# Buffer alignment in SBUF: probability buffers at multiples of 512 bytes, their transposed targets at multiples of 256, and one weight group moved to another pool

## The chip, the cores and the metric

The kernel runs on one core of a Trainium2 chip. Its five instruction streams are TensorE (PE, with its weight loads shown apart as PEld), VectorE (DVE), ScalarE (ACT), GpSimd (POOL) and SyncE (SP), which in this kernel does nothing but issue DMAs. Each stream runs its own instructions in order and waits for the others at semaphores. The metric is the time of one execution in microseconds of device time; runs are given by their median.

## The reference

One encoder layer over 2048 tokens of width 1024, in float32: `x + RMSNorm(W_out · ([A | B | M] * silu(z)))`. A, B and M all read one normalised input `h` through one combined projection.

```
h = rms_norm(x, norm_pre_w);  proj = h @ w_in
aq, ak, av, bqkv, ba, bb, mq, z = split(proj)
y_a = attention(rope(rms(aq)), rope(rms(ak)), av)        # 8 heads of 128, 2 key/value heads, 2048 x 2048
y_b = bidirectional gated DeltaNet(conv(bqkv), ba, bb)    # 4 heads, chunks of 64, both directions
y_m = attention(mq, keys and values from 256 memory tokens)  # 4 heads
x + rms_norm((concat(y_a, y_b, y_m) * silu(z)) @ w_out, norm_post_w)
```

The part that the change is about is the softmax attention: for each block of 128 queries and each head, scores of 128 x 2048, their softmax, and the product of the probabilities with the values.

## The kernel before, in words

Nearly every operation is recorded through a small wrapper, so that most of them stand at line 51 (L51) in the profile, and they are told apart by the names of their tiles. The weight loads issued by POOL stand at L77.

The kernel goes through its work in stages: the memory tokens' keys and values, the normalised tokens and the value projection (to about 122 us of the span), the key and query projections (to about 440), the projection and convolution of branch B (to about 700), the DeltaNet with the projections of `z` and `mq` between its steps (to about 1370), the attention (to about 2270) and the output projection (to the end).

Float32 precision is kept by splitting an operand in two halves, a high one and a low one: the float32 value rounded, and what is left. A product is then three matmuls (high·high, high·low, low·high).

**Attention.** There are 64 units (one head, 256 queries) of two blocks of 128 queries each, and 8 memory units of one block each, so 136 blocks. A block goes through these steps, and blocks overlap by up to five steps:

- PE computes the scores `sa` from the keys `K` and the queries `qa`; DVE takes their maximum (`mxa`); ACT exponentiates into the float32 tile `Pa`.
- `high()` has ACT write the high half of the normalised probabilities to `hla[:, 0]`; `low()` has DVE and POOL write the low half to `hla[:, 1]`. The tile `hl` (`hla`, for memory units `hlm`) is 128 partitions x 2 x 2048 half-precision numbers, 8 KB for each partition, in 3 buffers.
- SP then issues one transposing DMA at L1139, which writes the whole of `hla` into a quarter of the room `PT`, in 128 x 128 pieces. The four `PT` tiles hold two blocks each; PT0 and PT1 lie in the pool `hT`, PT2 and PT3 in the pool `late`.
- `value()` has PE multiply `PT` with the values `V` into `pva`; DVE multiplies the result by the gate (`gaa`), and SP stores it to the DRAM tensor `mix`.

PE, ACT and DVE run in an order written out by hand in this stage. SP's queue carries, besides the transposes, the loads of the queries (`qa<-qT`), of the gate (`gaa<-gate`), of memory queries (`M<-mqT`), and the stores (`mix<-gaa`).

**Pools.** The pool `hT` has one tag, `B16`, with 6 slots of 16 KB for each partition; in the course of the kernel they hold the raw weights (`wraw`), the turned memory tokens (`mT`), the turned tokens (`hT`), and in attention `K`, `V`, `M`, PT0, PT1, and parts of the output weights (`wo`) and of its input (`mhl`). Each is asked for with an alignment (`align_bytes`) of 128.

**Weight groups.** `load_w` loads a group of weight columns into `wraw`, squares it on ACT to find its scale (`wss`, `wsb`, a one-column matmul on PE, `wsc`), and splits it into half-precision parts (`wparts`) with ACT, DVE and POOL. Groups are counted by `n`. Group 0 has 272 columns (the values of A and the columns of `ba` and `bb`) and is loaded by SP while the memory groups are worked on; group 1 (256 columns) is the keys; groups 2 and on are queries and the rest. `parts` come from the pool `wpool` (tag `whb`, 2 buffers) for every third group beginning at 1, and otherwise from the pool `wp` (tag `whl`, 4 buffers), which the memory groups' parts (`whi`, `wlo`) use as well. Apart from the stages with pinned engines a scheduler orders the instructions of each engine, by its own estimate of when each is ready.

Of the kernel before, what the change touches and what calls it, by code (L numbers as in the profile page):

```python
# [11 lines left out]
F32 = mybir.dt.float32  # L12
F32R = mybir.dt.float32r
BF16 = mybir.dt.bfloat16
F16 = mybir.dt.float16
# [7 lines left out]
S = 2048  # L23
D = 1024
NMEM = 256
# [3 lines left out]
KC = D // 128  # L29
# [8 lines left out]
def hybrid_layer(ctx: ExitStack, tc: tile.TileContext, t: dict, out, dbg=None):  # L38
# [111 lines left out]
    def load_w(srcs, width, fac=(1.0,), fetch=None):  # L150


        n = wcount[0]
        wcount[0] += 1
        room = hpool.tile([128, 2, 4, width], F32, tag="B16", name="wraw", bufs=6, align_bytes=128)
        raws = [room[:, half] for half in range(2)]
        for half in range(2):
            for ap_to, ap_from in srcs(raws[half], half):
                (fetch or wdma)(ap_to, ap_from)
        pool, tag, bufs = (wpool, "whb", 2) if wpool is not None and n % 3 == 1 else (wp, "whl", 4)  # L160
        parts = [pool.tile([128, 2, 4, width], F16, tag=tag, name="wparts", bufs=bufs) for _ in range(2)]

        def small(name, dt=F32, pool=const2, bufs=4):
            return pool.tile([128, 1], dt, tag=name, name=f"{name}{n}", bufs=bufs)

        ss = [small(f"wss{i}") for i in range(2)]
        for half in range(2):
            A.activation(parts[half][:, 0].bitcast(BF16), raws[half], AF.Square, accum_out=ss[half])
        sb, y, e, sc = small("wsb", BF16), small("wy"), small("we", I32), small("wsc")
        V.tensor_tensor(sb, ss[0], ss[1], op=ALU.add)  # L170
        ps = tp_ps(f"wss{n}", (128, 1))
        T.matmul(ps, onesb, sb, start=True, stop=True)
        V.tensor_scalar(y.bitcast(I32), ps.bitcast(I32), -0.5, 1597463007.0, op0=ALU.mult, op1=ALU.add)
        V.tensor_scalar(e, y.bitcast(I32), 0x7f800000, None, op0=ALU.bitwise_and)
        V.tensor_scalar(sc.bitcast(I32), e, 1.0, float(14 << 23), op0=ALU.mult, op1=ALU.add)
        V.tensor_scalar(y.bitcast(I32), e, -1.0, float(240 << 23), op0=ALU.mult, op1=ALU.add)
        cs = [small("wc1", bufs=2)] * (len(fac) - 1) + [small("wc0", pool=const)]
        for c, f in zip(cs, fac):
            V.tensor_scalar(c, y, hcs, f, op0=ALU.mult, op1=ALU.mult)
        G.tensor_scalar(raws[1], raws[1], sc, None, op0=ALU.mult)  # L180
        A.activation(parts[0][:, 0], raws[0], AF.Copy, scale=sc)
        A.copy(parts[1][:, 0], raws[1])
        V.scalar_tensor_tensor(parts[0][:, 1], raws[0], sc, parts[0][:, 0], op0=ALU.mult, op1=ALU.subtract)
        G.tensor_tensor(parts[1][:, 1], raws[1], parts[1][:, 0], op=ALU.subtract)
        return [(w[:, 0], w[:, 1]) for w in parts], cs
# [3 lines left out]
    hpool = ctx.enter_context(tc.tile_pool(name="hT", bufs=1))  # L189
    p3 = ExitStack()  # L190
    wp = p3.enter_context(tc.tile_pool(name="wp", bufs=1))
# [7 lines left out]
    def tp_ps(name, shape=(128, 512)):  # L199
        return ps1.tile(list(shape), F32, tag="tp", name=name, bufs=4)  # L200

    hT = []
# [46 lines left out]
    wpool = w12.enter_context(tc.tile_pool(name="w12", bufs=1))  # L249

    def load_group(segs, fetch=None, fac=(1.0,)):

        def src(raw, half):
            o = 0
            for c0, n in segs:
                yield raw[:, :, o:o + n], t["w_in"][0, 512 * half:512 * half + 512, c0:c0 + n].rearrange("(k p) c -> p k c", p=128)
                o += n
        return load_w(src, sum(n for _, n in segs), fac, fetch)
# [12 lines left out]
    with tc.tile_pool(name="s0", bufs=1) as p:  # L271
# [15 lines left out]

        wmem = p.tile([128, D], F32, tag="wn", name="wmem")
        wpre = p.tile([128, D], F32, tag="wn", name="wpre")
        mTt = hpool.tile([128, 2, KC, NMEM], F32R, tag="B16", name="mT", bufs=6, align_bytes=128)  # L290
        mT = [mTt[:, i] for i in range(2)]
        xs, hm = [], []
        for j in range(2):
# [58 lines left out]
        for g in range(4):  # L352
# [2 lines left out]
                wav, (avcs,) = load_group([(1280, 256), (3072, 16)], dma)  # L355
            mem_group(g, wg)
            wg = nxt
        hT.extend(hpool.tile([128, 2, KC, 512], F16, tag="B16", name=f"hT{b}", bufs=6, align_bytes=128).rearrange("p i k c -> i p k c") for b in range(4))
        hs = {}

        def tok_norm(tb):
# [249 lines left out]
    wpool = None  # L611
# [48 lines left out]
                    (attention_loads, attention_slots)[b]()  # L660

    def slot(name, shape, dt=F32R):
        return hpool.tile(shape, dt, tag="B16", name=name, bufs=6, align_bytes=128)

    def late_slot(name, shape, dt=F32R):

        return late.tile(shape, dt, tag="L16", name=name, bufs=2, align_bytes=128)

    at = {}

    def attention_loads():

        at["k"] = slot("K", [128, 2, 2, S], F16)
        at["q0"] = wp.tile([128, 2, 2 * QW], F16, tag="wraw", name="qa0_0", bufs=1)
        dma(at["q0"], qT_d[0, :, :, 0:2 * QW])
        for k in range(4):
            dma(at["k"][:, 0, :, k * 512:(k + 1) * 512], kT_d[0, :, :, k * 512:(k + 1) * 512])

    def attention_slots():
        at["v"] = slot("V", [128, 2, TB, 256], F16)  # L680
        at["PT"] = [slot(f"PT{i}", [128, 2, 2, 16, 128], F16) for i in range(2)]
# [108 lines left out]
    with tc.tile_pool(name="s3a", bufs=1) as sv0:  # L790
        p = rows
# [24 lines left out]
        for hp in range(2):  # L816
            p = (sv0, sv1)[hp]
# [222 lines left out]
    late = ctx.enter_context(tc.tile_pool(name="late", bufs=1, side="right"))  # L1040
    ps2 = ctx.enter_context(tc.tile_pool(name="ps2", bufs=1, space=PSUM))
    p5 = ExitStack()
    p = p5.enter_context(tc.tile_pool(name="at", bufs=1))
# [7 lines left out]
    class Block:  # L1051
# [63 lines left out]
            V.reciprocal(sm[:, 2:3], sm[:, 2:3])  # L1115

        def high(self):
            hl = self.hl = p.tile([128, 2, S], F16, tag="hl", name=f"hl{self.nm}", bufs=3, align_bytes=128)
            P = self.P.rearrange("p a c -> p (a c)")
            if self.u["mem"]:  # L1120
                A.copy(hl[:, 0], P)
            else:
                A.activation(hl[:, 0], P, AF.Copy, scale=self.sm[:, 2:3])
            n = self.u["n"]
            if n in (2, 3) and len(PT) == n:
                PT.append(late_slot(f"PT{n}", [128, 2, 2, 16, 128], F16))
            self.pt = PT[n % 4][:, self.qb]
# [137 lines left out]
    for i in range(len(blocks) + LAG + 1):  # L1265
# [29 lines left out]
        for tb in range(2):  # L1295
            n = i - len(blocks) - 2 * tb
# [38 lines left out]
    with ExitStack() as es:  # L1335
        p = es.enter_context(tc.tile_pool(name="op", bufs=1))
        wo.append([late_slot(f"wo{i}_2", [128, 4, D]) for i in range(2)])
        wo.append([p.tile([128, 4, D], F32R, name=f"wo{i}_3") for i in range(2)])

# [98 lines left out]
```

## Time and profile before

| | |
|---|---|
| median of 3 runs | 2619.63 us (2618.19 to 2632.11) |
| the profiled execution | 2617.16 us, span 2615.4 us, mean granted clock of TensorE 0.972 |
| PE / PEld busy | 2393.9 us (92%) / 1626.0 us (62%) |
| DVE / ACT / POOL busy | 1754.0 us (67%) / 1285.6 us (49%) / 733.0 us (28%) |
| DMA | 440.08 MB, mean 168 GB/s, 857298 packets, 639744 of them under 512 B |
| largest idle times of PE by releaser | the transposing DMA into `PT` from `hla`: 96.0 us before `pva` |

PE is busy for 92% of the whole span. In the attention it is busy for less, and the 16 DMA engines are nearly always busy there (the row of DMA digits in the page has 9 in nearly every slice of this stage). A busy share of a window above 1 in the DMA column means that the packets' times overlap. SP's rows (SPq) are the time that its queue spent on issuing a DMA; they are not counted among the busy engines.

### The profile page before, as it was taken

How to read it: one execution, taken by the hardware profiler on the slowest of the kernel's cores; microseconds unless marked ns; L12 is line 12 of the kernel's file. 1: busy time of each engine (PE TensorE's matmuls, PEld its weight loads, DVE VectorE, ACT ScalarE, POOL GpSimd, SP SyncE). 2: the span in 40 equal slices, each digit the busy share in tenths (PEclk: the TensorE clock that was granted, in tenths of full speed). 3: DMA queues.
4: the chain of work that ended last, by engine and by line, in shares of the span. 5: the costliest groups of instructions: out<-in, count | busy, mean ns of one | idle time of the engine just before them, and what ended most of it. 6: DMA issues, size and time to landing. Idle time of an engine off the chain costs nothing.

```text
span 2615.4 us, 43108 instructions
## 1 busy us (share of the span) xinstructions
PE 2393.9 (92%) x15981; PEld 1626.0 (62%) x15981; DVE 1754.0 (67%) x3463; ACT 1285.6 (49%) x2496; POOL 733.0 (28%) x556
## 2 busy tenths in 40 slices
PE   7889999999999899999998888888888899999998
PEld 6778974555544356666645555555555555688887
DVE  7677769999568645545537777787887788442222
ACT  5633335544432245555636666676676677321110
POOL 2155331111202310210214444444455554200000
PEclk9999999999999999999999999998999999999999
DMA  6432223234585657767659999999999999953331
GB/s 206 152 92 86 65 62 101 73 113 131 192 254 126 191 166 215 235 207 233 215 173 221 211 212 208 213 213 205 195 213 211 210 207 203 218 164 95 96 95 51
DMA packets 857298, 440.08 MB, mean 168 GB/s; under 512 B 639744, under 2 KB 813184, under 8 KB 856832
## 3 DMA queue, kind: packets, MB, share of 16 engines
q1 hardware_dynamic: 844640, 394.32, 63.1%
q0 software_dynamic: 12448, 43.00, 4.9%
q8 instruction: 126, 2.06, 0.3%
q14 instruction: 84, 0.69, 0.1%
HBM read 186.62 MB, written 108.00 MB: 113 GB/s over the span
## 4 chain that ended last, share of the span: by engine, by line
PE 21%; issue 15%; POOL 12%; DMA 5%; DVE 2%; ACT 1%; SPq 1%; POOLq 0%; DVEq 0%; ACTq 0%
PE o L51 12%; POOL hla L51 7%; POOL Pa L51 4%; PE z L51 3%; DMA PT<-hla 2%; PE pva L51 1%; PE sa L51 1%; DMA xx<-bx 1%; DVE mxa L51 1%; DMA Od<-oo 1%; POOL wo L51 1%; DMA wor<-in_w_out 1%; DVE hla L51 1%; DMA ft<-FT 0%; PE sm L51 0%
## 5 line engine op out<-in xcount | busy, mean ns | idle before, releaser
L51 PE MATMUL pva<-PT,V 128*128 128x256 f16 x3072 | 399.0, 282 | 115.4 <-DMA PT<-hla 96.0
L51 PEld LDWEIGHTS <-wparts 128*128 128x128 f16 x3072 | 294.0, 98 | 326.4 <-issue 16.4
L51 PEld LDWEIGHTS <-V 128*128 128x128 f16 x3072 | 305.6, 101 | 225.0 <-issue 96.4
L51 ACT ACTIVATE Pa<-sa,mxa,undo 128x1024 f32<-128x1024 f32 x256 | 305.8, 1198 | 223.7 <-DVE sma L51 186.0
L51 DVE TENSOR_REDUCE mxa<-sa 128x1 f32<-128x1024 f32 x256 | 309.6, 1217 | 140.6 <-PE sa L51 139.5
L51 PE MATMUL sa<-K,qa 128*128 128x512 f16 x1536 | 388.4, 390 | 5.1 <-ACT Pa L51 3.6
L51 PE MATMUL z<-hT,wparts 128*128 128x512 f16 x1536 | 372.4, 383 | 0.0
L51 PE MATMUL o<-wo,mhl 128*128 128x512 f32 x1416 | 325.5, 391 | 3.9 <-ACT wo L51 2.6
L51 PEld LDWEIGHTS o<-wo,mhl 128*128 128x128 f32 x1416 | 265.4, 188 | 63.7 <-ACT wo L51 3.4
L51 ACT ACTIVATE hla<-Pa,sma 128x2048 f16<-128x2048 f32 x128 | 255.5, 1996 | 37.2 <-DMA PT<-hla 34.2
L51 DVE SCALAR_TENSOR_TENSOR hla<-Pa,sma,hla 128x1536 f16<-128x1536 f32 x128 | 258.4, 2018 | 5.9 <-ACT hla L51 5.9
L51 PE MATMUL b<-hT,wparts 128*128 128x512 f16 x1152 | 256.8, 379 | 0.0
L51 PEld LDWEIGHTS <-hT 128*128 128x128 f16 x2304 | 226.2, 99 | 38.3 <-ACT hT L51 5.9
L51 POOL TENSOR_TENSOR Pa<-Pa,sma 128x512 f32<-128x512 f32 x128 | 134.5, 1051 | 406.6 <-ACT hla L51 398.4
L51 PEld LDWEIGHTS <-qa 128*128 128x128 f16 x1536 | 154.7, 101 | 146.2 <-issue 21.6
L51 POOL TENSOR_TENSOR hla<-Pa,hla 128x512 f16<-128x512 f32 x128 | 229.4, 1792 | 9.4
L51 PE MATMUL q<-wparts,hT 128*128 128x256 f16 x1920 | 214.9, 274 | 0.0
L51 POOL TENSOR_SCALAR wraw<-wraw,wsc 128x1024 f32<-128x1024 f32 (+1 forms) x22 | 67.5, 3067 | 335.8 <-DVE wy L51 256.8
L51 DVE TENSOR_TENSOR mhl<-mr,mhl 128x2048 fp32r<-128x2048 f32 (+1 forms) x16 | 35.1, 2192 | 177.3 <-ACT mhl L51 177.2
L51 DVE SCALAR_TENSOR_TENSOR y<-xb,convw,y 128x512 f32<-128x512 f32 x192 | 145.5, 773 | 1.7
L51 ACT CAST mhl<-mr 128x2048 fp32r<-128x2048 f32 (+1 forms) x16 | 29.2, 1826 | 225.9 <-PE o L51 211.1
L77 POOL DMA_DIRECT2D gate<-zg x64 | 35.5, 555 | 367.9 <-DVE zg L51 197.8
(317 smaller groups left out, 3274.6 us busy)
## 6 DMA issues: line engine op xcount, KB each, us to landing
xx<-bx SPq DMA_DIRECT2D x64, 512.0 KB, 5.0
wraw<-in_w_in POOLq DMA_DIRECT2D x42, 512.0 KB, 5.3
gate<-zg POOLq DMA_DIRECT2D x64, 256.0 KB, 4.0
NI<-nit SPq DMA_DIRECT2D x32, 512.0 KB, 3.5
mr<-mix SPq DMA_DIRECT2D x13, 1024.0 KB, 5.9
x<-in_x SPq DMA_DIRECT2D x16, 512.0 KB, 4.5
qT<-qo SPq DMA_DIRECT2D x32, 256.0 KB, 2.5
qa<-qT SPq DMA_DIRECT2D x32, 256.0 KB, 3.5
```

Source lines behind the costliest of these rows:

```text
L51: ins = f(*args, **kw)
L77: nc.gpsimd.dma_start(to, of)
```

## The change

Four kinds of edit, none of which changes an instruction's shape, type or count:

- The probability tile `hl` is asked for at multiples of 512 bytes in place of 128. In the built program its three buffers move from the addresses 171648, 179840 and 188032 (each 128 above a multiple of 512) to 171008, 179200 and 187392 (multiples of 512).
- All tiles of the tag `B16` are asked for at multiples of 512. They were at 384 above a multiple of 512 and are at multiples of 512 now, among them PT0 and PT1 (33152 and 82304 before, 33280 and 82432 after).
- The pool `late` is asked for at multiples of 256. PT2 and PT3 move from 196480 and 212864 (128 above a multiple of 256) to 196352 and 212736 (multiples of 256, at 256 above a multiple of 512).
- Group 0 of the weights, whose 272 columns take 4352 bytes for each part, goes to the pool `wpool` (tag `whb`), and group 1 to the pool `wp` (tag `whl`); groups 4, 7 and 10 stay in `wpool`. The four slots of `whl` shrink from 4352 to 4096 bytes, the two of `whb` grow from 4096 to 4352. Other tiles move by a few hundred bytes with that.

```
-        room = hpool.tile([128, 2, 4, width], F32, tag="B16", name="wraw", bufs=6, align_bytes=128)
+        room = hpool.tile([128, 2, 4, width], F32, tag="B16", name="wraw", bufs=6, align_bytes=512)
...
-        pool, tag, bufs = (wpool, "whb", 2) if wpool is not None and n % 3 == 1 else (wp, "whl", 4)
+        pool, tag, bufs = (wpool, "whb", 2) if wpool is not None and n in (0, 4, 7, 10) else (wp, "whl", 4)
...
-        mTt = hpool.tile([128, 2, KC, NMEM], F32R, tag="B16", name="mT", bufs=6, align_bytes=128)
+        mTt = hpool.tile([128, 2, KC, NMEM], F32R, tag="B16", name="mT", bufs=6, align_bytes=512)
...
-        hT.extend(hpool.tile([128, 2, KC, 512], F16, tag="B16", name=f"hT{b}", bufs=6, align_bytes=128).rearrange("p i k c -> i p k c") for b in range(4))
+        hT.extend(hpool.tile([128, 2, KC, 512], F16, tag="B16", name=f"hT{b}", bufs=6, align_bytes=512).rearrange("p i k c -> i p k c") for b in range(4))
...
     def slot(name, shape, dt=F32R):
-        return hpool.tile(shape, dt, tag="B16", name=name, bufs=6, align_bytes=128)
+        return hpool.tile(shape, dt, tag="B16", name=name, bufs=6, align_bytes=512)
...
     def late_slot(name, shape, dt=F32R):
-        return late.tile(shape, dt, tag="L16", name=name, bufs=2, align_bytes=128)
+        return late.tile(shape, dt, tag="L16", name=name, bufs=2, align_bytes=256)
...
-            hl = self.hl = p.tile([128, 2, S], F16, tag="hl", name=f"hl{self.nm}", bufs=3, align_bytes=128)
+            hl = self.hl = p.tile([128, 2, S], F16, tag="hl", name=f"hl{self.nm}", bufs=3, align_bytes=512)
```

From the second half of the key and query projections on, every engine has the same instructions in the same order as before. Ahead of that (the first 230 us of the span) the two groups' pools change when the scheduler finds room for them, and so the order. In the rows below a number behind a name tells copies of a tile apart; `wss_362` is the one-column matmul for the scale of group 0, `mem_220`, `mem_283`, `mem_376` and `mem_427` are the four memory groups, `tp_*` are transposes of the first normalised tokens `h_505` and `h_507`. On PE, the scale's matmul and the first transposes stood inside the fourth memory group before:

```order
 L51 MATMUL mem_427<-whi,mT 128x256 x2
-L51 LDWEIGHTS onesb
-L51 MATMUL wss_362<-wsb_357,onesb 128x1
-L51 MATMUL tp_0_536<-ident,h_505 128x128 x4
-L51 MATMUL tp_1_543<-ident,h_505 128x128 x4
-L51 MATMUL tp_0_550<-ident,h_507 128x128 x4
-L51 MATMUL tp_1_557<-ident,h_507 128x128 x4
```

Now they stand at the beginning of the second one:

```order
 L51 MATMUL mem_220<-mT,whi 128x256 x2
 L51 MATMUL mem_220<-mT,wlo 128x256
+L51 LDWEIGHTS onesb
+L51 MATMUL wss_362<-wsb_357,onesb 128x1
 L51 MATMUL mem_283<-mT,whi 128x256 x2
+L51 MATMUL tp_0_536<-ident,h_505 128x128 x4
+L51 MATMUL tp_1_543<-ident,h_505 128x128 x4
+L51 MATMUL tp_0_550<-ident,h_507 128x128 x4
```

With them the products of the value projection (`av_621`), which were behind the whole fourth memory group, begin inside it. On ACT, the two squares of group 0 that feed this scale stood beside the casts of the fourth memory group's weights, and now they stand ahead of the statistics of the fourth token tile (`x_515`):

```order
 L51 CAST mT<-tp_m_1_190 128x4x128
+L51 ACTIVATE wparts,wss_353<-wraw 128x1088
+L51 ACTIVATE wparts,wss_354<-wraw 128x1088
 L51 ACTIVATE jk_x_517,ss_509<-x_515 128x1024
 L51 CAST whi<-mraw 128x1024 x2
```

On DVE the sum of these squares (`wsb_357`) moves likewise, from behind the last split of memory weights to a place ahead of `nsm`, the scale of the norm weights, from which the first tokens `h` follow.

## The prediction

> **What bounds the kernel now.** I read the time windows first, to see in which stage PE, the busiest engine, has room at all. In each row the window and its length are followed by the busy time of PE, PEld, DVE, ACT and POOL (with counts), the granted clock of PE, the DMA share and GB/s:
>
> ```profile
> 122.00:200.00 78.00, 70.59 (x622) 62.50 (x620) 53.10 (x113) 23.17 (x37) 37.76 (x27) 0.93 0.34 100
> 1400.00:1700.00 300.00, 249.15 (x1643) 165.40 (x1642) 235.69 (x306) 202.22 (x280) 134.26 (x88) 0.94 1.07 212
> 1700.00:2000.00 300.00, 255.84 (x1678) 168.48 (x1677) 241.02 (x312) 209.91 (x270) 147.70 (x96) 0.93 1.05 207
> 2000.00:2270.00 270.00, 244.28 (x1610) 164.94 (x1609) 205.09 (x263) 180.33 (x204) 128.24 (x85) 0.97 1.09 210
> 2400.00:2615.00 215.00, 207.41 (x908) 170.00 (x906) 60.55 (x121) 25.80 (x30) 0.00 (x0) 0.99 0.26 81
> ```
>
> In attention (1400 to 2270 us) PE is busy 749.3 of 870 us, so 120.7 us are open there, while the DMA column is full at 207 to 212 GB/s. In the output stage PE is short of full by 7.6 us in 215. So attention has to be looked at, and in it the transposing DMA, which everything edited here feeds or receives. The view of the tile `PT` gives its issues (issue time min/median/max, first and last start) and who waited for it:
>
> ```profile
> L1139 SPq DMA_TRANSPOSE PT<-hla x128: 4682/5105/7675, 1372.6 to 2254.4; - x128
>   PE pva L51: 96.0, 42
>   PEld L51: 61.2, 29
>   ACT hla L51: 34.7, 23
>   PE pvm L51: 4.4, 3
> DMA to landing us min/median/max: 6.6/7.4/10.7
> ```
>
> PE stands idle for 96.0 + 4.4 = 100.4 us until a transpose lands, most of the 120.7. Landing follows the issue closely: 7.4 us after its start, of which 5.1 us is the issue itself. So what fills SP's queue? The timeline of SP (start, issue time):
>
> ```profile
> 2084.77 5.06 SPq L1139 DMA_TRANSPOSE PT<-hla  x1
> 2089.92 0.53 SPq L51 DMA_DIRECT2D mix<-gaa  x1
> 2090.62 4.80 SPq L1139 DMA_TRANSPOSE PT<-hla  x1
> 2095.52 0.53 SPq L51 DMA_DIRECT2D gaa<-gate  x1
> 2096.15 0.55 SPq L51 DMA_DIRECT2D qa<-qT  x1
> 2096.79 5.53 SPq L1139 DMA_TRANSPOSE PT<-hla  x1
> 2102.42 0.52 SPq L51 DMA_DIRECT2D mix<-gaa  x1
> 2103.04 4.88 SPq L1139 DMA_TRANSPOSE PT<-hla  x1
> 2108.01 0.54 SPq L51 DMA_DIRECT2D gaa<-gate  x1
> 2108.64 5.08 SPq L1139 DMA_TRANSPOSE PT<-hla  x1
> ```
>
> SP goes from issue to issue with no more than 0.1 to 0.2 us between them. Four blocks take 2108.64 - 2084.77 = 23.87 us, 5.97 for each: transposes 5.06 + 4.80 + 5.53 + 4.88 = 20.27, plain DMAs 2.67, gaps 0.93. PE in the same stretch:
>
> ```profile
> 2095.38 1.47 PE L51 MATMUL pva<-PT,V 128*128 128x256 f16 x12
> 2096.68 1.46 PE L51 MATMUL sa<-K,qa 128*128 128x512 f16 x6
> 2097.98 1.47 PE L51 MATMUL pva<-PT,V 128*128 128x256 f16 x12
> 2104.09 1.47 PE L51 MATMUL pva<-PT,V 128*128 128x256 f16 x12 [0.73 <-DMA PT<-hla]
> ```
>
> A group of 6 score matmuls and one of 12 value matmuls take 2097.98 - 2095.38 = 2.60 us together; a block has 24 value matmuls (x3072 `pva` over 128 blocks), so two such pairs, 5.2 us. SP needs 5.97 for what PE does in 5.2; SP's queue bounds attention by 0.77 us a block, and PE meets it in waits like the last row's 0.73. Over 128 blocks that is 98.6 us, and the tile's view has 96.0. The sums agree.
>
> **What sets a transpose's 4.8 to 5.1 us** decides the forecast. Either SP makes the descriptors at that rate, or the DMA engines take the pieces at that rate and hold SP back. Only the second can depend on where `hla` and `PT` lie. The trace separates them, by two short windows of the DMA view. The first lies inside one transpose that SP had a free road for, 1720.6 to 1725.4 (the high rates at its left are the tail of the one before and a load); the second, 1785 to 1789, is one where a load ahead had held the queue up, and the engines then ran through what had piled up:
>
> ```profile
> GB/s 294 286 355 350 358 231 9 0 73 209 230 226 207 211 218 198 215 222 213 215 220 218 222 215 215 220 222 218 215 218 215 222 222 209 224 213 220 218 215 222
> DMA packets 3734, 1.04 MB, mean 217 GB/s; under 512 B 3606, under 2 KB 3734, under 8 KB 3734
> GB/s 26 20 18 13 184 289 289 297 289 289 292 289 287 284 289 282 287 284 282 294 292 289 287 292 289 287 294 287 289 289 287 297 289 289 292 221 31 108 82 102
> DMA packets 3650, 0.95 MB, mean 237 GB/s; under 512 B 3622, under 2 KB 3650, under 8 KB 3650
> ```
>
> The same tiles at the same addresses go at 215 to 222 GB/s when SP feeds them as it issues, and at 284 to 297 GB/s when descriptors lie ready. A transpose is 128 x 2 x 2048 x 2 B = 1.05 MB: at 218 GB/s 4.81 us, which is what the undisturbed issues take (4.80, 4.88); at 289 it would be 3.63. So the engines are not at their limit in the steady state, with the old addresses, and the pace is that of the queue that feeds them.
>
> [...]
>
> **The change, part by part.**
>
> *`hla` and `PT` at new addresses.* 136 transposes, no instruction more or less. From the last rows: SP's 4.8 to 5.1 us stay, so 0 of the 100.4 us of waits comes back. Its bounds: below, the rate of the second window in all transposes, worked out with the rivals (-100 us); above, an unknown cost of both sides meeting on the same multiples, up to 0.3 us a block, the spread between the four issues' mean (5.07) and a typical disturbed one (5.53 is 0.46 above it, two thirds of that): +41 us. I take 0, being nearest to the rows with the same tiles.
>
> *The other `B16` tiles* (`wraw`, `hT`, `K`, `V`, `M`, `wo`, `mhl`) are moved by 128 bytes. Their DMAs lie beside PE's work: up to 1400 us beside projections, then in the output stage beside the 207.41 of 215 us; without that cover they would at most fill its 7.6 us. I take 0; ends -5 and +5.
>
> *Group 0's scale goes earlier.* The waits of the first 125 us (total, times, longest), and four rows of timelines:
>
> ```profile
> DVE wsb L51 <- ACT wparts L51: 4.9, 2, 4.5
> PE av L51 <- ACT hT L51: 4.9, 3, 3.2
> PE mem L51 <- POOL wlo L51: 1.9, 1, 1.9
> PE mem L51 <- DVE wlo L51: 1.8, 1, 1.8
> PE wss L51 <- DVE wsb L51: 1.5, 1, 1.5
> PE av L51 <- DVE p2mmk L51: 1.2, 1, 1.2
> ...
> 9.42 3.02 SPq L51 DMA_DIRECT2D wraw<-in_w_in  x4
> 19.17 1.22 DVE L51 TENSOR_REDUCE nsm<-wpre 128x1 f32<-128x1024 f32 x1 [0.16 <-DMA wpre<-in_norm_pre_w]
> 20.55 1.06 ACT L51 ACTIVATE jk_x<-x 128x1024 bf16<-128x1024 f32 x1 [3.70 <-DMA x<-in_x]
> 40.97 1.11 ACT L51 ACTIVATE wparts<-wraw 128x1088 bf16<-128x1088 f32 x1 [2.47 <-PE mem L51]
> ...
> DMA to landing us min/median/max: 4.3/6.4/7.3
> ```
>
> The last row is that of `wraw`: issued by 12.44 us, it has landed by 19.7 at the latest. The squares (2 x 1.11 us and their read-outs, 2.6) can then run in the 3.70 us in which ACT waits for a token tile, and end between 19.2 and 22.3. DVE's `wsb` stands ahead of `nsm` now; queued behind it are `nsm`, the first `h` and the split `wlo` for which PE waits 1.8 us already. So up to 22.3 - 19.17 = 3.1 us later there. In return PE's 1.5 us and DVE's 4.5 us for this scale go, transposes fill PE inside the memory groups, and the 4.9 + 1.2 us of waits at the value projection are open to be filled. Ends: -7.6 (1.5 + 4.9 + 1.2) and +3.1. I take their middle, -2. What of this lies behind 122 us passes through the 7.41 us that PE is idle in the window of 122 to 200; a square or two less of ACT's work there (1.06 us each, group 3's, which move behind the keys) is worth at most those 7.41, and I take 0, since other conversions stand there still.
>
> Sum: 0 + 0 - 2 + 0 = -2 us on the profiled execution, whose time is 2617.16 with a span of 2615.4 us: 2615. The median of the three runs shown is 2619.63, 2.5 above it, so a median of 2617.
>
> **The rivals.**
>
> *A: the addresses do set the pace (faster).* If SP's issue is held back by the engines in a way that the second window doesn't show, and the new addresses let all transposes run at its rate, an issue takes 3.63 in place of 4.81 and a block on SP 5.97 - 1.18 = 4.79 us, below PE's 5.2. PE is the bound then, and the waits of 100.4 us go, less what else is late on the way (`hla` from ACT, DVE and POOL): 70 to 100 us, some 2532. For it: 100 us of waits have this one cause, and an exact cost per piece would give sharp rates like these. Against it: 289 GB/s at old addresses. [...]
>
> *B: only the disturbed transposes get shorter (faster, a little).* If the engines work off a pile faster, what is above 4.80 in the four issues (5.07 - 4.80 = 0.27) could go in part: 0.27 x 136 = 37 us at most, half of it 18: 2599.
>
> *C: the new addresses collide (slower).* The buffers `hla` and the targets PT0 and PT1 now begin at the same offset from multiples of 512 (0 and 0); before they were 256 apart (128 and 384). If reads and writes of the same partitions meet more often, the steady 218 GB/s fall; SP has no slack, so each 0.1 us on an issue is 13.6 us. From 0.1 us on it decides; at 0.3 us the time is 2658. Nothing in the trace speaks for it except that the queue is full.
>
> *D: the early scale waits longer (slower or nothing).* With `wraw` landing last in a full queue, 3.1 us plus a second delay of the same size in the next memory group: +6, 2623, which is within what can be told.
>
> **How the numbers follow.** A measurement of this kernel tells about 0.5% (13 us) from no change, given the spread of the runs shown. No change, the likeliest, with D: 0.53; its own range is 2608 to 2630. A: 0.25. B: 0.09. C: 0.13. So faster by over 0.5% is A and B, 0.34; slower is C, 0.13. The range reaches down to 2525, which leaves out a third of A (0.08), and up to 2635, which leaves out nearly all of C (0.11).
>
> **What would show it.** Right: issues at L1139 still 4.8 to 5.1 us, steady stretches still at 215 to 222 GB/s, PE still idle some 96 us before `pva` for `PT`; the scale of group 0 near 25 us and the value projection a few us earlier. Wrong towards A: issues near 3.6 to 4 us, 280 GB/s and more throughout the attention, waits for `PT` nearly gone and PE at 5.2 us a block. Wrong towards C: issues above 5.2 us and waits above 110. The forecast rests on one inference, that the steady rate is SP's own; a higher steady rate at the same descriptors would refute it.

## The result, and the profile after

The changed kernel takes 2542.56 us (median of 4 runs, 2535.68 to 2552.2) against 2619.14 us; the ratio is 0.970, interval 0.965 to 0.974. That is 76.6 us less. The likeliest case of the prediction (no change, 2617 us) did not come; rival A (some 2532 us, 70 to 100 us less) did.

The profiled execution after took 2535.68 us, with a span of 2533.9, which is 81.5 us below the one before. All of that lies in attention. One window for each kernel holds the stage, from the first transpose on (before, then after; columns as in the prediction):

```profile
1373.00:2271.00 898.00, 774.66 (x5064) 513.11 (x5061) 703.42 (x910) 612.20 (x776) 425.27 (x279) 0.95 1.07 210
```
```profile
1373.00:2190.00 817.00, 748.68 (x5052) 502.98 (x5051) 720.83 (x911) 610.93 (x777) 424.85 (x280) 0.98 1.05 231
```

The stage is 81 us shorter. PE's idle time in it falls from 123.3 to 68.3 us, 55 us. The other 26 us are PE's busy time: the matmuls took 774.7 us at a granted clock of 0.95 and take 748.7 at 0.98. (The second window has 12 records fewer of some 5060, worth 2 us; over the whole execution PE's busy time fell by as much, from 2393.9 to 2368.4 us.) The view of `PT` after the change:

```profile
L1139 SPq DMA_TRANSPOSE PT<-hla x128: 3845/4228/6751, 1373.2 to 2173.4; - x128
  PE pva L51: 53.2, 31
  PEld L51: 29.1, 16
  ACT hla L51: 7.8, 5
  PE pvm L51: 1.8, 2
DMA to landing us min/median/max: 5.5/6.5/10.3
```

The issue's median went from 5.1 to 4.2 us, and PE waits 53.2 + 1.8 = 55.0 us for `PT` in place of 100.4. SP's timeline after the change, four blocks:

```profile
2097.10 4.79 SPq L1139 DMA_TRANSPOSE PT<-hla  x1
2101.99 0.53 SPq L51 DMA_DIRECT2D mix<-gaa  x1
2102.62 4.06 SPq L1139 DMA_TRANSPOSE PT<-hla  x1
2106.78 0.53 SPq L51 DMA_DIRECT2D gaa<-gate  x1
2107.40 4.95 SPq L1139 DMA_TRANSPOSE PT<-hla  x1
2112.46 0.52 SPq L51 DMA_DIRECT2D mix<-gaa  x1
2113.08 4.04 SPq L1139 DMA_TRANSPOSE PT<-hla  x1
2117.22 0.53 SPq L51 DMA_DIRECT2D gaa<-gate  x1
2117.85 4.12 SPq L1139 DMA_TRANSPOSE PT<-hla  x1
```

(2117.85 - 2097.10) / 4 = 5.19 us a block, against 5.97 before: that is PE's own 5.2 us. PE is busy in all of this stretch, so SP no longer holds it up there:

```profile
2097.10:2117.85 20.75, 20.75 (x145) 14.01 (x144) 20.47 (x26) 17.34 (x21) 11.58 (x8) 1.00 1.15 250
```

SP has no room either: it still goes from issue to issue with 0.1 us between them, so the two are level. The DMA view of 2110 to 2115 shows the rate that the prediction had seen only after a pile-up, now as the ordinary one:

```profile
GB/s 8 10 10 8 10 8 197 295 283 293 285 293 291 293 289 289 293 285 293 291 293 289 287 295 285 293 291 293 289 287 291 343 377 385 181 254 291 287 291 293
```

### The profile page after: what moved, and what is told of

The parts are those of the page before. It is cut to its first block, busy times and chain, and to the rows that moved or that the text cites. A ratio compares the mean times of both kernels' runs of the same rounds, so it can differ in the third digit from the quotient of the medians.

```text
span 2533.9 us, 43094 instructions
## 1 busy us (share of the span) xinstructions
PE 2368.4 (93%) x15973; PEld 1617.2 (64%) x15981; DVE 1782.4 (70%) x3463; ACT 1284.8 (51%) x2496; POOL 731.6 (29%) x556
## 4 chain that ended last, share of the span: by engine, by line
PE 20%; issue 12%; POOL 11%; DVE 5%; DMA 5%; ACT 2%; SPq 1%; POOLq 0%; DVEq 0%; ACTq 0%
PE o L51 12%; POOL hla L51 6%; POOL Pa L51 4%; PE z L51 3%; DVE mxa L51 2%; DMA PT<-hla 2%; DVE hla L51 1%; PE sa L51 1%; DMA Od<-oo 1%; PE pva L51 1%; DMA xx<-bx 1%; DMA ft<-FT 1%; POOL wo L51 1%; DMA wor<-in_w_out 1%; DVE mxm L51 0%
## 5 line engine op out<-in xcount | busy, mean ns | idle before, releaser
L51 PE MATMUL pva<-PT,V 128*128 128x256 f16 x3072 | 386.3, 277 | 56.2 <-DMA PT<-hla 53.2
L51 PE MATMUL sa<-K,qa 128*128 128x512 f16 x1536 | 378.9, 383 | 11.4 <-ACT Pa L51 9.3
L51 DVE SCALAR_TENSOR_TENSOR hla<-Pa,sma,hla 128x1536 f16<-128x1536 f32 x128 | 273.6, 2137 | 3.0 <-ACT hla L51 2.9
```

The source lines that it names most:

```text
L51: ins = f(*args, **kw)
```

## The experiments

Four kernels first took the change apart: its order, its sources, its targets. In what follows "the source" is the probability tile `hla`, which a transpose reads, and "the target" is `PT`; a source theory has only the place that is read count, a target theory only the place that is written.

**The exchange of the pools alone.** The kernel before, with this edit only:

```
-        pool, tag, bufs = (wpool, "whb", 2) if wpool is not None and n % 3 == 1 else (wp, "whl", 4)
+        pool, tag, bufs = (wpool, "whb", 2) if wpool is not None and n in (0, 4, 7, 10) else (wp, "whl", 4)
```

> The kernel before with the pools of weight groups 0 and 1 exchanged, as in the change; all alignments are those of before (the probability tile and its targets at 128 above a multiple of 256). If the gain comes from the addresses, this does nothing: 2617 us give or take 8, issues of the transposes 4.7 to 5.1 us, and the early stage moves by less than 5 us. If the new order of the first 230 us is worth something by itself, up to 8 us of the gain of 77 us show here (2609 to 2612).

Measured: 2623.47 us, ratio 1.000 (0.9984 to 1.0016).

```profile
L1139 SPq DMA_TRANSPOSE PT<-hla x128: 4718/5143/7226, 1382.0 to 2261.5; - x128
  PE pva L51: 93.8, 42
```

The order of the first 230 us is worth nothing that can be measured here; the gain comes with the addresses.

**The source alone back at 128.** The changed kernel, with a filler of 128 bytes ahead of the tile (in the kernels with other offsets the filler has their size):

```
         def high(self):
+            if self is blocks[0]:
+                p.tile([128, 32], F32, tag="shift", name="shift")
-            hl = ... bufs=3, align_bytes=512)
+            hl = ... bufs=3, align_bytes=32)
```

> The changed kernel with the probability tile alone put back to 128 above a multiple of 512; the targets PT and all else stay at multiples of 256. [...] Target theory (only where the pieces are written counts): nothing is lost, about 2543 us and 289 GB/s. [...]

Measured: 2620.66 us, ratio 0.9989 (0.9972 to 1.0005). All of the gain is gone, the target theory's 2543 us did not come, and the issues are those of before (median 5.16 us against 5.11):

```profile
L1141 SPq DMA_TRANSPOSE PT<-hla x128: 4684/5162/7738, 1374.8 to 2258.2; - x128
  PE pva L51: 112.9, 47
```

**The targets alone back at 128.** The changed kernel with an alignment of 128 for the tags `B16` and `L16` in place of 512 and 256 (which puts them at 128 above a multiple of 256 again); a filler of 128 bytes keeps the source at a multiple of 256.

```
-        return hpool.tile(shape, dt, tag="B16", name=name, bufs=6, align_bytes=512)
+        return hpool.tile(shape, dt, tag="B16", name=name, bufs=6, align_bytes=128)
...
-        return late.tile(shape, dt, tag="L16", name=name, bufs=2, align_bytes=256)
+        return late.tile(shape, dt, tag="L16", name=name, bufs=2, align_bytes=128)
```

> The changed kernel with the targets PT (and the other 16 KB tiles) put back to 128 above a multiple of 256; the probability tile starts at a multiple of 256 (256 above a multiple of 512). Source theory: nothing is lost, about 2543 us, 289 GB/s, issues near 4.0 us. Target theory: about 2617 us, 218 GB/s. It also shows whether a multiple of 256 is enough for the source.

Measured: 2547.07 us, ratio 0.9712 (0.9696 to 0.9727), an interval inside that of the whole change.

```profile
L1141 SPq DMA_TRANSPOSE PT<-hla x128: 3933/4322/7269, 1383.5 to 2184.4; - x128
  PE pva L51: 39.2, 25
```

The attention, from the first to the last transpose, takes 800.9 us here and 800.2 after the change. For the transposes only the source counts. Its start here is 256 above a multiple of 512, so a multiple of 256 was enough: issues of 4.32 us at the median, against 4.23 from multiples of 512.

**The source at 192.** The changed kernel with a filler of 192 bytes ahead of the tile.

> The changed kernel with the probability tile at 192 above a multiple of 512, targets at multiples of 256. [...] Theory of a flat penalty (any source off a multiple of 256 means two reads, or SP makes such descriptors more slowly): as at 128, about 2617 us and 218 GB/s. Target theory: 2543 us.

Measured: 2622.91 us, ratio 1.0005 (0.9992 to 1.0018).

```profile
L1141 SPq DMA_TRANSPOSE PT<-hla x128: 4679/5153/7682, 1375.4 to 2257.0; - x128
  PE pva L51: 99.3, 44
```

That is the time at 128 (2620.66 us), and the issue's median is that at 128 too (5.15 us against 5.16): at these two starts the penalty is the same.

**Who pays: the DMA engines, or SP as it makes the descriptors?** Both would look the same in a transpose. A kernel of its own leaves the layer out and moves data only; it was executed once.

```
for nm, off in (("zero", 0), ("atthirtytwo", 32), ("atsixtyfour", 64), ("athalf", 128), ("atthreequarters", 192)):
    for i in range(3):
        turn(target, src[:, off // 2:off // 2 + 2 * S])      # transposing DMA of 1 MB
...
for size in (256, 512, 1024, 2048):                          # plain stores in pieces of this size
    for off in (0, 128, 192):
        ...
```

> A kernel that leaves out the whole layer and only moves data on SP's queue: three 1 MB transposes on end from each of five starts of the source (0, 32, 64, 128, 192 above a multiple of 512) into aligned targets, three into targets at 128; 4 MB of loads followed by three transposes, from 0 and from 128; then plain 1 MB stores from SBUF in pieces of 256, 512, 1024 and 2048 B that start at 0, 128 or 192, and plain loads in pieces of 256 to 1024 B to targets at 0 or 128. Theory E, the DMA engines read a piece that starts off a multiple of 256 in one read more, at a fixed 4.7 ns for a piece (18.8 against 14.1 ns, in which the offset of 192 cost no more than that of 128): transposes at 289 GB/s from 0 and at 218 from all four others, 289 into the shifted targets; stores of 1024 B pieces at about 42.5 against 47.4 ns for a piece (385 against 346 GB/s), those of 512 B lose more, those of 2048 B about 5%; loads lose nothing. Theory P, SP makes the descriptors of a transpose more slowly for such a start and the engines don't mind: the transposes are the same as in E, but stores of 512 B and more lose nothing, since the engines and not SP pace them. [...]

The timeline of SP, three transposes in each row (the last row is the source at 0 into targets at 128):

```profile
5.28 12.40 SPq L29 DMA_TRANSPOSE Tzero<-src  x3
17.73 14.79 SPq L29 DMA_TRANSPOSE Tatthirtytwo<-src  x3
32.56 14.68 SPq L29 DMA_TRANSPOSE Tatsixtyfour<-src  x3
47.29 14.91 SPq L29 DMA_TRANSPOSE Tathalf<-src  x3
62.24 14.82 SPq L29 DMA_TRANSPOSE Tatthreequarters<-src  x3
77.10 12.43 SPq L29 DMA_TRANSPOSE Ttargethalf<-src  x3
```

12.4 us from 0, 14.7 to 14.9 from every other start, 12.4 into shifted targets. For one transpose that is 4.13 against 4.93 us of issue, 0.8 us less, where 289 in place of 218 GB/s alone would make it 1.2. The DMA view of 9 to 17 us, three transposes from 0, shows why:

```profile
GB/s 291 289 293 289 287 288 106 3 18 239 292 292 288 289 291 289 292 292 288 289 288 288 288 291 288 289 279 72 1 32 265 287 289 291 289 293 291 288 289 291
```

From 0 the engines stand idle for about half a microsecond between two transposes (a slice is 0.2 us), though nothing else is in the queue. The plain stores decide between the engines and SP. The last number of each row is GB/s; the pairs of rows are pieces of 256, 512, 1024 and 2048 B, from 0 and then from 128 or 192:

```profile
141.20:147.00 5.80, 0.00 (x0) 0.00 (x0) 1.00 1.28 290
153.00:160.00 7.00, 0.00 (x0) 0.00 (x0) 1.00 1.00 217
168.00:172.00 4.00, 0.00 (x0) 0.00 (x0) 1.00 1.15 348
176.00:178.00 2.00, 0.00 (x0) 0.00 (x0) 1.00 0.99 290
189.00:194.00 5.00, 0.00 (x0) 0.00 (x0) 1.00 1.09 386
196.00:199.50 3.50, 0.00 (x0) 0.00 (x0) 1.00 1.03 343
205.50:210.50 5.00, 0.00 (x0) 0.00 (x0) 1.00 1.05 408
212.00:214.00 2.00, 0.00 (x0) 0.00 (x0) 1.00 1.04 388
```

Sixteen engines at these rates spend, on a piece, 16 x size / rate: 14.1 and 18.9 ns, 23.5 and 28.2, 42.4 and 47.8, 80.3 and 84.5. The differences are 4.8, 4.7, 5.3 and 4.1 ns, whatever the size. The windows from 128 or 192 are laid behind a fast stretch: the two stores of 256 B from 0 are 2.1 MB, 7.2 us at 290 GB/s, and this rate lasts longer, over pieces off a multiple too:

```profile
141.00:150.00 9.00, 0.00 (x0) 0.00 (x0) 1.00 1.28 290
```

SP can't be the cause of the slower rate: pieces of 256 B from 0 were served at 290 GB/s, one in 14.1 ns for each engine, and those of 2048 B ask for one in 80.3 to 84.5 ns. So theory E holds for what is read from SBUF: an extra of some 4.7 ns for each piece, paid by the engines or on their way to SBUF, which no run separates. That it is one read more is not shown. P falls.

Theory E also had loads lose nothing, and that is not borne out. Each row has KB and the median time from issue to landing in us; "zero" is a target at 0, "athalf" one at 128:

```profile
ldquarterKzero<-far SPq DMA_DIRECT2D x2, 1024.0 KB, 5.9
ldquarterKathalf<-far SPq DMA_DIRECT2D x2, 1024.0 KB, 7.1
```

The loads of 512 B pieces landed after 5.6 and 6.3 us, those of 1024 B after 5.2 and 5.8: later into 128 in all three sizes. There are two loads of each, in one execution, so the cost for a piece stays open.

The same kernel repeats what misled the prediction. It issued 4 MB of loads and then transposes from 128. The DMA view of 126 to 132 us, at the end of the loads:

```profile
GB/s 355 410 410 382 362 280 336 225 150 152 276 292 288 290 290 288 290 292 290 292 288 290 290 288 290 292 290 292 288 290 226 87 203 232 220 207 213 218 215 217
```

After the load, pieces from 128 go at 288 to 292 GB/s for some 3 us, and then at 218. A fast stretch behind a blocked queue thus occurs with a source that costs 18.9 ns a piece in the long run, and the stores above show the same behind stores from 0. What makes it fast is not shown: no run takes the reading apart from the writing.

**What is left.** 55 us of waits for `PT` remain. Three kernels asked whether the plain loads in SP's queue are their cause. The first issues query, memory-query and memory-gate loads from POOL:

```
-        dma(q, qT_d[h, :, :, q0:q0 + 2 * QW])
+        wdma(q, qT_d[h, :, :, q0:q0 + 2 * QW])
```

> The changed kernel with the loads of queries (qa), of memory queries (M) and of the memory units' gates (gam) issued by POOL in place of SP, 56 DMAs of about 0.55 us. If the 55 us that PE still waits for PT come from transposes that stand behind such loads in SP's queue (issues of 5 to 6.7 us after qa, M and gam, about 4.0 after a store), about half of these waits go: 2510 to 2525. Rival: POOL's 0.55 us for each and its waits for a free buffer delay the low halves of the probabilities by as much: 2540 to 2555, no gain.

Measured: 2564.16 us, ratio to the kernel before 0.978 (0.976 to 0.980), slower than the change itself and outside both ranges. The view of `qa` shows one price, POOL waiting in its order until the score matmuls release a query buffer:

```profile
  POOL qa L77: 61.5, 24
```

That this wait is the reason is not shown: the transposes land later too (median 6.9 us against 6.5), as they do in the next kernel.

The second issues them from ACT (`A.dma_start` in the same places):

> The changed kernel with the loads of queries, memory queries and the memory units' gates issued by ACT in place of SP. With POOL as issuer it lost 20 us, as POOL waited 61 us in its own order for the query buffers to come free. Theory: ACT has more slack (it waits 130 us for sums anyway) but in its written order it waits for the same buffers, and the probabilities behind it come late: 2545 to 2570. Rival: the buffers are free by ACT's turn, transposes run without loads ahead of them: 2510 to 2535.

Measured: 2570.44 us, ratio 0.981 (0.979 to 0.983).

```profile
L1139 SPq DMA_TRANSPOSE PT<-hla x128: 3888/4323/7904, 1377.4 to 2205.0; - x128
  PE pva L51: 67.7, 27
DMA to landing us min/median/max: 5.5/7.0/12.5
```

The theory's range held, but not by its reason: every load of `qa` follows the instruction ahead of it on ACT within 0.1 us, and transposes land later (median 7.0 us against 6.5, maximum 12.5 against 10.3) though none of the moved loads stands ahead of them in SP's queue. What delays them there is not shown. The third leaves 30 of the query loads out:

```
     def load_q(nm, h, q0):
+        if "kept" in at:
+            return at["kept"]
```

> The changed kernel with 30 of the 31 query loads of the attention left out: all units after the first use the queries that were loaded once (so the outputs of other heads and rows are not those of the layer). If the 55 us that PE still waits for PT after the change are due to transposes that stand behind plain loads in SP's queue, this takes a large part of them away: PE waits of 20 to 40 us for PT, 2505 to 2530 us. Rival: what is left is the pace of transposes and of the engines that write the probabilities, and loads are only where the wait is met: 2538 to 2550 us, waits of 50 us.

Measured: 2524.13 us, ratio 0.963 (0.961 to 0.965).

```profile
  PE pva L51: 36.5, 21
```

Without these loads the waits fall by 17 us and the time by 18 against the changed kernel. Leaving the loads out takes away both their place in SP's queue and their work on the engines. As another queue for the loads gained nothing, the part they have in what is left is likelier their work on the engines; no run takes the two apart. In the built program `qa` and `gaa` still begin at 64 above a multiple of 256 after the change, and no kernel aligned them. No kernel that computes the layer came out faster than the changed one.

## Why the prediction was right or wrong

The measured 2542.56 us lies between the prediction's 2525 and 2635, but that is no success of its mechanism. The range reached so far down only to take in most of rival A, which had a chance of 0.25; the single forecast, 2617, is 74 us off.

- *SP's queue bounds attention, 5.97 us a block against PE's 5.2:* right. When an issue got shorter, the block went to 5.19 us, PE's own, in the stretch shown; over the whole stage, 136 blocks, it went from 6.5 to 5.9 us.
- *The pace of a transpose is SP's own, so the addresses give 0 us:* wrong, and this is the step that failed: the term for `hla` and `PT` was put at 0 of the 100.4 us of waits, and 45.4 came back, with 26 us of PE's busy time beside them. The step took the 284 to 297 GB/s behind a held-up queue for what the engines can do with the old addresses. The steady 218 GB/s were the engines' limit: the source put back to 128 alone brings back the issues, the time and the rate (210 to 225 GB/s from 1724.2 to 1726 us of its profile), and the engines' extra of some 4.7 ns shows in plain stores where SP sets no pace. That only an engine-side limit can depend on addresses was the author's premise; the plain stores, slower by 4.1 to 5.3 ns a piece from 128 and 192, fit it. The row chosen to decide between the two measured a different state.
- *The size of the extra:* starts at 32, 64, 128 and 192 measure alike (14.79, 14.68, 14.91 and 14.82 us for three transposes, against 12.40 from 0), so in these runs it did not grow with the distance from the multiple.
- *Rival A's working:* the mechanism is what happened, and each term is a little smaller. An issue takes 4.2 us at the median in place of 3.63. The loads among the transposes are not all of it: three on end, with nothing between, took 4.13 us each, as the engines stood idle between them, which the sum left out. The waits for `PT` fall by 45.4 us, not by 70 to 100. What made up for it is a term that the prediction did not have: PE's busy time fell by 26 us with the higher granted clock. So the closeness of 2532 to the measured time is in part luck. That the clock rose because the stalls went is not tested apart.
- *Rival B*, a gain in the disturbed transposes only, and *rival C*, a collision, did not come: the shortest issues fell as well (4682 to 3845 ns), and no issue time of the view rose.
- *The early order, -2 us:* the first transpose starts at 1373.2 us against 1372.6, so it is +0.6 in one profile each. The steps were there. DVE's wait for the squares and PE's for the scale went from 4.9 and 1.5 us to 0.3 each, and DVE's split `wlo` came later, as the waits of the first 125 us after the change show (1.8 us before, and 1.9 for POOL's split, which are gone). That is rival D's delay, made up for by the rest:

```profile
PE wss L51 <- DVE wsb L51: 0.3, 1, 0.3
DVE wsb L51 <- ACT wparts L51: 0.3, 1, 0.3
PE mem L51 <- DVE wlo L51: 5.2, 2, 4.0
PE av L51 <- ACT hT L51: 0.6, 1, 0.6
```

  The gain at the value projection was given back behind it, at the key projection, where PE's waits for DVE grew. From 118 us on before, and from 112 us on after, to 365 us:

```profile
PE qt L51 <- DVE qr L51: 9.9, 2, 7.4
```
```profile
PE qt L51 <- DVE qr L51: 14.4, 3, 7.8
```
- *The other `B16` tiles, 0 us between -5 and +5:* perhaps a little too small. With the new order the first transpose starts at 1382.0 and 1383.5 us in the two kernels whose tiles lie at 128 above a multiple of 256, and at 1373.2 to 1377.4 in those with aligned tiles shown here. Some 5 to 10 us may be the aligned tiles' gain, and as much the new order's loss; that loads landed later into targets at 128 would fit, but single profiles don't settle it, and the time of the kernel with unaligned targets can't be told from that of the whole change.

## What to carry to other kernels

Where a DMA reads SBUF in small pieces, a transposing DMA above all, let the tile begin at a multiple of 256 bytes (starts at 0 and 256 above a multiple of 512 were fast here, those at 32, 64, 128 and 192 slow): with pieces of 256 B the engines took 14.1 ns for each in place of 18.9. The place of a transpose's target made no difference (12.43 us for three into targets at 128, 12.40 into targets at 0); for targets of loads that isn't settled. A rate seen just behind a blocked queue is no measure of what the engines sustain (288 to 292 GB/s for some 3 us here, then 218); test a limit in the steady state, or with the one address changed. When the queue that bounds a stage gets faster, work out anew what bounds it (here PE's 5.2 us a block) before hoping for the rest.

## What the runs showed of the hardware

- A piece read from SBUF at 128 or 192 above a multiple of 256 bytes cost the DMA engines 4.1 to 5.3 ns more in plain stores, for pieces of 256 to 2048 B; in transposes the issue grew alike for starts at 32, 64, 128 and 192 (14.68 to 14.91 us for three, against 12.40).
- Behind loads, and behind stores from a multiple of 256, pieces off a multiple went at the faster rate for about 2 to 3 us (288 to 292 GB/s) before they fell to 218.
- Between two transposes from a multiple of 256 the engines stood idle for about 0.5 us, so that an issue took 4.13 us where 289 GB/s alone would give 3.63.
- Loads of 1 MB landed later into SBUF targets at 128 than at 0: 7.1 against 5.9 us, 6.3 against 5.6, 5.8 against 5.2 (two of each, in one execution).
- The matmuls of the attention took 774.7 us at a granted clock of 0.95 and 748.7 us at 0.98, in the kernel with fewer stalls: a third of the gain of this change came that way.
- With query loads moved from SP's queue to ACT's the transposes landed later (median 7.0 against 6.5 us): a separate queue did not shield them in this run.
